# Padding 32 bytes shorter and a stated place for the first weight sums, in a transformer layer on one core

## The chip, the cores and the metric

The kernel runs on one core of one Trainium2 chip. The metric is the device time of one execution in microseconds (us); lower is better. The engines are named PE (matrix products; PEld is its loading of weights), DVE, ACT and POOL (elementwise work), and SP, which here only issues transfers.

## The reference

One decoder layer over 512 tokens of width 2048, all in float32:

```python
h = rmsnorm(x, norm_attn_g)
proj = h @ w_in                      # q, k, v of two attention groups
o_a = swa_attention(rmsnorm(q_a), rmsnorm(k_a), v_a, sinks, rel_bias)
o_b = stick_breaking_attention(q_b, k_b, v_b)
mix = concat(rmsnorm(o_a, swa_out_g), rmsnorm(o_b, sb_out_g))
x = x + mix @ w_out                  # 2048 x 2048
h = rmsnorm(x, norm_mlp_g)
u = h @ w_up                         # 2048 x 8192
x = x + square(relu(u)) @ w_down     # 8192 x 2048
```

## The kernel before

**Products.** Each float32 operand is split into two parts, hi (the value cast to float32r, on ACT, L91) and lo (the rest, a subtraction of two tiles on DVE, L92). A product is then three matmuls, hi by hi, hi by lo and lo by hi. A matmul has two operands in on-chip memory: 128 columns of weights, which PE loads first, and a moving operand of 256 or 512 columns.

**Stages.** Projection of k and v, then q, k and v of the two attention groups, with the attention itself worked in between; the output projection; the up projection (from 741 us); the down projection (from 1407 us). In all projections ahead of the up projection a matmul has 512 moving columns, and there are 2,496 of them (nine groups of 192, eight of 96).

**Up projection.** 32 column groups, each of 8 steps: steps 0 to 6 have 21 matmuls, step 7 has 24, 171 in all (L809 to L811), with 256 moving columns. Weights are `hi_u`, `lo_u`; the moving operand is `h2h`, `h2l`, one pair of tiles for each step. POOL sums columns of the raw weights `st_u` into `s_u` (L779), four instructions for two steps (fast matrix products need such sums). DVE makes `lo_u` from `st_u` and `s_u`, and does most of `u_finish` of the group before (L823 to L845), in program order. PE, DVE and POOL each run their instructions in the order written.

**Down projection.** 16 turns (`cj`), each of 7 products of 24 matmuls with 512 moving columns (L1053 to L1055), 2,688 in all. Weights are `ad`, the moving operand is `hi_d`, `lo_d`. POOL makes four sums of raw weights for a turn, T1 to T4, each in two halves (L931). Half of the tiles of `st_d`, and T1 of turn 0, are asked for in the last column group of the up projection:

```python
if k == 1:
    d_load(0, 0)
    d_act(0, ORDER[0])
elif k == 4:
    d_sum(0, "T1")
elif k == 6:
    d_split(0)
```

The other `ad` of turn 0 are issued on SP behind the stores of the group before (`ac<-ah`, `ac<-al`, L848), the second of which needs `al` (L845).

**Where tiles lie.** On-chip memory is a stack from the left (pools `const`, `wst`, `whl`, `sm`, `big`, later `aba`, `rwa`, `ew`) and one from the right (`once` to `wk` in attention, `h2_0` to `h2_5`, `sp`, later `rwb`, `t3`, `abb`). Small tiles of the pool `const` come first on the left, and tiles that nothing uses (`pad_left`, `pad_small`, `pad_right`) set where the large ones begin. In the built program before, the large tiles on the left begin 32 bytes past a multiple of 512 in each partition (the first of `wst` at 3104), those on the right at a multiple of 512. So:

- projections ahead of the up projection: both operands on the left, both 32 past;
- up projection: weights on the left (32 past); `h2` of steps 0 to 5 on the right (0), of steps 6 and 7 on the left (32 past);
- down projection: moving operand on the left (32 past); `ad` of the first product of each turn on the left (32 past, pool `aba`), of the other six on the right (0, pool `abb`);
- `mp_k` (L338, L339): weights `bo` in `const`, 32 past, and moving operands on the right (0).

Slices of these operands begin at multiples of 512 bytes in their tiles.

Of the kernel before, what the change touches and what calls it, by code (L numbers as in the profile page):

```python
# [12 lines left out]
F32 = mybir.dt.float32  # L13
# [7 lines left out]
P = 128  # L21
# [37 lines left out]
def hymba_layer(ctx: ExitStack, tc: tile.TileContext, x, norm_attn_g, w_in, q_norm_g, k_norm_g,  # L59
                sinks, rel_bias, swa_out_g, sb_out_g, w_out, norm_mlp_g, w_up, w_down, sel, eye, out):  # L60
    nc = tc.nc
    x, out = x[0], out[0]
# [4 lines left out]
    const = ctx.enter_context(tc.tile_pool(name="const", bufs=1))  # L67
# [293 lines left out]
        return o  # L361

    oscr = dram.tile([2 * 8, P, T], F32, name="oscr")
    const.tile([P, 32], F32, name="pad_left")
    sm.tile([P, 32], F32, tag="pad", bufs=1, name="pad_small")
    S = [once.tile([P, T], F32, name=f"S{b}") for b in range(2)]

# [389 lines left out]


    wu = w_up.rearrange("(k p) c -> p k c", p=P)
    raws, sums, parts_u = {}, {}, {}  # L760

    def u_load(i):
        if i < G * KP // 2:
# [5 lines left out]
    def u_sums(i):  # L769
        if i < G * KP // 2:  # L770
            w = raws[i]
            s_ = sp.tile([P, 2, 4, P], F32, tag="s", name=f"s_u{i}")
            if i % (KP // 2) == PLAIN // 2:
                w, s_ = w[:, 0:1], s_[:, 0:1]
            for o, a, b, op in ((s_[:, :, 0], w[:, :, 0], w[:, :, 2], ALU.add),
                                (s_[:, :, 2], w[:, :, 1], w[:, :, 0], ALU.subtract),
                                (s_[:, :, 1], s_[:, :, 0], w[:, :, 1], ALU.subtract),
                                (s_[:, :, 3], w[:, :, 3], s_[:, :, 1], ALU.subtract)):
                nc.gpsimd.tensor_tensor(out=o, in0=a, in1=b, op=op)  # L779
            sums[i] = s_  # L780

    def u_split(i):
# [68 lines left out]
    def u_step(i, ps, finishing):  # L851
        if i % 2 == 0:
            u_load(i // 2 + 4)
            u_sums(i // 2 + 2)
        u_split(i + 2)
        u_products(i, ps)
        if finishing is not None:
            next(finishing, None)

    def u_begin(c2):  # L860
        if c2 == 3:
            for i in range(4):
                u_load(i)
            u_sums(0)
            u_split(0)
            u_sums(1)
# [12 lines left out]
    def u_banks(g):  # L879
        pool, tag = ((pa, "pa"), (pp, "pp"))[g % 2]  # L880
        return [pool.tile([P, 512], F32, tag=tag, name=f"ps_u{g}{m}") for m in range(4)]
# [26 lines left out]
    def d_load(cj, r):  # L908
        if cj < 2 * NC:
            c, j = divmod(cj, 2)  # L910
            for h in range(2):
                pool = rwa if (4 * cj + 2 * r + h) % 6 < 2 else rwb
                st = pool.tile([P, 2, 1024], F32, tag="rw", name=f"st_d{cj}{r}{h}")
                nc.sync.dma_start(out=st, in_=wd[1 - r, :, 4 * c + 2 * h:4 * c + 2 * h + 2,
                                                 j * 1024:(j + 1) * 1024])
                for n in range(2):
                    raw[cj, f"B{r + 1}{n + 1}", h] = st[:, :, n * 512:(n + 1) * 512]

    def d_act(c, i):
        if c < NC:  # L920
            a = (aba if i == ORDER[0] else abb).tile([P, 2, 4, HP], F32R, tag="a", name=f"ad{c}{i}")
            nc.sync.dma_start(out=a.bitcast(F32), in_=ac[c][i])
            act[c, i] = a

    def d_sum(cj, name):
        if cj < 2 * NC:
            a, b = {"T1": ("B12", "B11"), "T2": ("B22", "T1"), "T3": ("B22", "B12"), "T4": ("B21", "T2")}[name]
            for h in range(2):
                pool, tag = (t3, "t3") if name == "T3" else (wst, "st")
                o = pool.tile([P, 2, 512], F32, tag=tag, name=f"{name}_{cj}{h}")  # L930
                nc.gpsimd.tensor_tensor(out=o, in0=raw[cj, a, h], in1=raw[cj, b, h], op=ALU.subtract)  # L931
                raw[cj, name, h] = o

    def d_split(q):
        if q < 14 * NC:
            cj, s = divmod(q, 7)
            for h in range(2):
                hi = whl.tile([P, 2, 512], F32R, tag="hi", name=f"hi_d{q}{h}")
                lo = whl.tile([P, 2, 512], F32R, tag="lo", name=f"lo_d{q}{h}")
                split(raw[cj, D_PRODUCTS[s][2], h], hi, lo)  # L940
                parts_d[q, h] = hi, lo
# [51 lines left out]
    for g in range(1, G):  # L993
        finishing = u_finish(g - 1, ps, ew)
        ps = u_banks(g)
        for k in range(KP):
            if g == G - 1:
                if k == 1:
                    d_load(0, 0)
                    d_act(0, ORDER[0])  # L1000
                elif k == 4:
                    d_sum(0, "T1")
                elif k == 6:
                    d_split(0)
            u_step(g * KP + k, ps, finishing)
# [6 lines left out]
    for cj in range(2 * NC):  # L1012
# [7 lines left out]
        for s, (name, ai, _, b, more) in enumerate(D_PRODUCTS):  # L1020
# [22 lines left out]
            a = act[c, ai]  # L1043

            at_end = q == 14 * NC - 1
            for h, tt in sorted(((h, tt) for h in range(2) for tt in range(2)), key=lambda x: x[::-1] if at_end else x):
                bh, bl = parts_d[q, h]
                ts = slice(tt * P, (tt + 1) * P)
                o = banks[b][tt]
# [39 lines left out]
```

## Time and profile before

| | |
|---|---|
| median of 3 runs | 2043.79 us (2041.43 to 2044.12) |
| the profiled execution | 2043.11 us, of which the span from first to last instruction is 2041.0 us |
| busy in the span | PE 2004.0, DVE 1626.8, POOL 1020.3, ACT 1014.5 us |
| mean granted PE clock | 0.996 |

The times are the kernel's whole device time; 2.1 us of the profiled one lie outside the span. Busy time of PE overlaps from one matmul to the next, so that a PE that is always busy can still run its matmuls at a slower or faster pitch (time from one start to the next).

### The profile page before, as it was taken

How to read it: one execution, taken by the hardware profiler on the slowest of the kernel's cores; microseconds unless marked ns; L12 is line 12 of the kernel's file. 1: busy time of each engine (PE TensorE's matmuls, PEld its weight loads, DVE VectorE, ACT ScalarE, POOL GpSimd, SP SyncE). 2: the span in 40 equal slices, each digit the busy share in tenths (PEclk: the TensorE clock that was granted, in tenths of full speed). 3: DMA queues.
4: the chain of work that ended last, by engine and by line, in shares of the span. 5: the costliest groups of instructions: out<-in, count | busy, mean ns of one | idle time of the engine just before them, and what ended most of it. 6: DMA issues, size and time to landing. Idle time of an engine off the chain costs nothing. (4 is left out here: it accounts for less than half of the span.)

```text
span 2041.0 us, 31132 instructions
## 1 busy us (share of the span) xinstructions
PE 2004.0 (98%) x11748; PEld 1725.3 (85%) x11748; DVE 1626.8 (80%) x2034; ACT 1014.5 (50%) x1676; POOL 1020.3 (50%) x904
## 2 busy tenths in 40 slices
PE   8999999999999999999999999998999999999998
PEld 7887787778677889999999999997788888888887
DVE  4378646665775578999999999998989999999987
ACT  6267534544553565555555555554543333333343
POOL 0014332222320127777777777775756556655654
PEclk9999999999999999999999999999999999999999
DMA  6742332223345555665656565656756557456351
GB/s 220 123 129 85 100 93 81 73 92 111 107 134 186 168 166 182 203 203 183 203 182 205 182 205 182 206 182 264 273 223 227 177 216 267 155 226 258 145 186 62
DMA packets 213914, 350.30 MB, mean 172 GB/s; under 512 B 9779, under 2 KB 154372, under 8 KB 206596
## 3 DMA queue, kind: packets, MB, share of 16 engines
q1 hardware_dynamic: 211216, 345.02, 49.8%
q10 hardware_dynamic: 2548, 3.30, 1.3%
q8 instruction: 92, 1.51, 0.3%
q14 instruction: 58, 0.48, 0.1%
HBM read 270.16 MB, written 78.12 MB: 171 GB/s over the span
## 5 line engine op out<-in xcount | busy, mean ns | idle before, releaser
L811 PE MATMUL ps_u<-h2h,lo_u 128*128 128x256 f32 x1824 | 515.9, 283 | 6.3 <-DVE lo_u L92 6.3
L810 PE MATMUL ps_u<-h2l,hi_u 128*128 128x256 f32 x1824 | 514.7, 282 | 2.4 <-DVE h2l L92 2.4
L809 PE MATMUL ps_u<-h2h,hi_u 128*128 128x256 f32 x1824 | 514.8, 282 | 0.1
L1053 PE MATMUL ps_d<-hi_d,ad 128*128 128x512 f32 x896 | 353.4, 394 | 3.4 <-ACT U L969 1.6
L1054 PE MATMUL ps_d<-lo_d,ad 128*128 128x512 f32 x896 | 353.4, 394 | 1.2 <-DVE lo_d L92 1.2
L1055 PE MATMUL ps_d<-hi_d,ad 128*128 128x512 f32 x896 | 353.2, 394 | 0.0
L811 PEld LDWEIGHTS ps_u<-h2h,lo_u 128*128 128x128 f32 x1824 | 346.7, 190 | 7.5 <-DVE lo_u L92 6.7
L810 PEld LDWEIGHTS ps_u<-h2l,hi_u 128*128 128x128 f32 x1824 | 346.6, 190 | 2.9 <-DVE h2l L92 2.8
L809 PEld LDWEIGHTS ps_u<-h2h,hi_u 128*128 128x128 f32 x1824 | 346.6, 190 | 0.3 <-ACT h2h L91 0.3
L779 POOL TENSOR_TENSOR s_u<-st_u 128x256 f32<-128x256 f32 (+1 forms) x256 | 200.1, 801 | 252.3 <-DVE lo_u L92 181.2
L92 DVE TENSOR_TENSOR lo_d<-T,hi_d 128x1024 fp32r<-128x1024 f32 x128 | 241.4, 1899 | 38.1 <-ACT hi_d L91 37.4
L931 POOL TENSOR_TENSOR T<-st_d,T 128x1024 f32<-128x1024 f32 x64 | 169.1, 2645 | 201.0 <-DVE lo_d L92 198.5
L91 ACT CAST hi_d<-T 128x1024 fp32r<-128x1024 f32 x128 | 134.4, 1051 | 203.0 <-PE ps_d L1055 177.6
L92 DVE TENSOR_TENSOR lo_u<-st_u,hi_u 128x384 fp32r<-128x384 f32 (+1 forms) x256 | 218.2, 853 | 4.4 <-ACT hi_u L91 4.3
L1053 PEld LDWEIGHTS ps_d<-hi_d,ad 128*128 128x128 f32 x896 | 167.9, 187 | 44.6 <-ACT U L969 2.1
L92 DVE TENSOR_TENSOR lo_d<-st_d,hi_d 128x1024 fp32r<-128x1024 f32 x96 | 193.5, 2028 | 13.7 <-ACT hi_d L91 13.2
L1054 PEld LDWEIGHTS ps_d<-lo_d,ad 128*128 128x128 f32 x896 | 168.0, 188 | 42.0 <-DVE lo_d L92 2.0
L1055 PEld LDWEIGHTS ps_d<-hi_d,ad 128*128 128x128 f32 x896 | 168.0, 187 | 40.1
L92 DVE TENSOR_TENSOR lo_u<-s_u,hi_u 128x512 fp32r<-128x512 f32 x224 | 178.1, 795 | 1.0 <-ACT hi_u L91 1.0
L91 ACT CAST hi_u<-s_u 128x512 fp32r<-128x512 f32 x224 | 138.5, 618 | 78.7 <-POOL s_u L779 78.6
L91 ACT CAST hi_d<-st_d 128x1024 fp32r<-128x1024 f32 x96 | 100.6, 1050 | 152.2 <-PE ps_d L1055 140.6
L779 POOL TENSOR_TENSOR s_u<-st_u,s_u 128x256 f32<-128x256 f32 (+1 forms) x128 | 167.8, 1311 | 10.0
(223 smaller groups left out, 3825.7 us busy)
## 6 DMA issues: line engine op xcount, KB each, us to landing
st_u<-in_w_up SPq DMA_DIRECT2D x128, 512.0 KB, 4.5
st_d<-in_w_down SPq DMA_DIRECT2D x64, 1024.0 KB, 8.3
ad<-ac SPq DMA_DIRECT2D x56, 1024.0 KB, 5.1
ac<-ah SPq DMA_DIRECT2D x32, 896.0 KB, 6.3
ac<-al SPq DMA_DIRECT2D x32, 896.0 KB, 6.6
st_qk<-in_w_in SPq DMA_DIRECT2D x64, 256.0 KB, 3.0
st_o<-in_w_out SPq DMA_DIRECT2D x32, 512.0 KB, 4.5
st_qa<-in_w_in SPq DMA_DIRECT2D x16, 512.0 KB, 4.1
```

Source lines behind the costliest of these rows:

```text
L91: nc.scalar.copy(out=hi, in_=st)
L92: nc.vector.tensor_tensor(out=lo, in0=st, in1=hi.bitcast(F32), op=ALU.subtract)
L779: nc.gpsimd.tensor_tensor(out=o, in0=a, in1=b, op=op)
L809: nc.tensor.matmul(o, wh[:, a], hh[:, b], start=first, stop=False, skip_group_check=True)
L810: nc.tensor.matmul(o, wh[:, a], hl[:, b], start=False, stop=False, skip_group_check=True)
L811: nc.tensor.matmul(o, wl[:, a], hh[:, b], start=False, stop=(k == KP - 1), skip_group_check=True)
L931: nc.gpsimd.tensor_tensor(out=o, in0=raw[cj, a, h], in1=raw[cj, b, h], op=ALU.subtract)
L1053: nc.tensor.matmul(o, al, bh[:, kk], start=first, stop=False, skip_group_check=True)
L1054: nc.tensor.matmul(o, al, bl[:, kk], start=False, stop=False, skip_group_check=True)
L1055: nc.tensor.matmul(o, ar, bh[:, kk], start=False, stop=end, skip_group_check=True)
```

## The change

```diff
-    const.tile([P, 32], F32, name="pad_left")
+    const.tile([P, 24], F32, name="pad_left")
...
-    raws, sums, parts_u = {}, {}, {}
+    raws, sums, parts_u, last_sum = {}, {}, {}, [None]
...
-                nc.gpsimd.tensor_tensor(out=o, in0=a, in1=b, op=op)
+                last_sum[0] = nc.gpsimd.tensor_tensor(out=o, in0=a, in1=b, op=op)
...
                 elif k == 4:
-                    d_sum(0, "T1")
+                    with tc.issue_after(last_sum[0].ins):
+                        d_sum(0, "T1")
```

The pad has 24 words in place of 32. Every tile of the left stack behind it lies 32 bytes lower: the first of `wst` at 3072, and all large tiles, left and right, begin at multiples of 512. `bo` lies ahead of the pad and stays. The number of instructions of each engine stays the same.

The second part moves two instructions on POOL. Below is POOL's order in the last column group; `s_u126` and `s_u127` are the sums for steps 4 and 5, and 6 and 7, of that group; T1_00 and T1_01 are the halves of T1 of turn 0.

```order
-L931 TENSOR_TENSOR T1_00_15576<-st_d000_15477 128x1024
 L779 TENSOR_TENSOR s_u126_15440<-st_u126_15303 128x2x128 x2
 L779 TENSOR_TENSOR s_u126_15440<-s_u126_15440,st_u126_15303 128x2x128
 L779 TENSOR_TENSOR s_u126_15440<-st_u126_15303,s_u126_15440 128x2x128
-L931 TENSOR_TENSOR T1_01_15578<-st_d001_15479 128x1024
 L779 TENSOR_TENSOR s_u127_15511<-st_u127_15369 128x128 x2
 L779 TENSOR_TENSOR s_u127_15511<-s_u127_15511,st_u127_15369 128x128
 L779 TENSOR_TENSOR s_u127_15511<-st_u127_15369,s_u127_15511 128x128
+L931 TENSOR_TENSOR T1_00_15576<-st_d000_15477 128x1024
+L931 TENSOR_TENSOR T1_01_15578<-st_d001_15479 128x1024
 L931 TENSOR_TENSOR T3_00_15731<-st_d010_15713,st_d000_15477 128x1024
 L931 TENSOR_TENSOR T2_00_15820<-st_d010_15713,T1_00_15576 128x1024
```

The two halves of T1 stood ahead of the sums of steps 4 and 5 and ahead of those of step 6; now both stand behind them, and T3 and T2 follow directly.

ACT keeps its order; two of its casts for the second product of the down projection get one more wait:

```order
 L91 CAST hi_d00_15639<-st_d000_15477 128x1024 [waits PE_49]
 L91 CAST hi_d01_15643<-st_d001_15479 128x1024 [waits PE_49]
-L91 CAST hi_d10_15735<-T1_00_15576 128x1024 [waits PE_49,Activation_49]
-L91 CAST hi_d11_15739<-T1_01_15578 128x1024 [waits DVE_49,PE_49]
+L91 CAST hi_d10_15735<-T1_00_15576 128x1024 [waits PE_49,Activation_49,Pool_49]
+L91 CAST hi_d11_15739<-T1_01_15578 128x1024 [waits DVE_49,PE_49,Pool_49]
 L822 COPY p1_31_15769<-ps_u310_15436 128x256 [waits PE_49]
 L91 CAST hi_d20_15824<-T3_00_15731 128x1024 [waits DVE_49,PE_49,Pool_49]
```

`hi_d10` and `hi_d11` now wait for POOL by name. On PE, DVE, ACT and SP each instruction stands where it stood.

## Rows read from the trace of the kernel before

**Rows 1.** Windows of 100 us: busy us and instructions (x) of each engine, granted PE clock.

```profile
core 0: us, PE busy (x) PEld busy (x) DVE busy (x) ACT busy (x) POOL busy (x), PEclk, DMA share, GB/s
...
800.00:900.00 100.00, 100.00 (x845) 100.00 (x844) 90.46 (x123) 58.09 (x95) 74.58 (x79) 1.00 0.64 208
...
1200.00:1300.00 100.00, 100.00 (x838) 99.59 (x837) 90.45 (x123) 56.23 (x94) 74.17 (x77) 1.00 0.59 191
...
1700.00:1800.00 100.00, 100.00 (x431) 80.61 (x430) 93.64 (x77) 37.84 (x36) 55.89 (x20) 1.00 0.62 230
```

**Rows 2.** Timeline of PE, down projection: start, length; 24 matmuls from row to row.

```profile
1605.31 0.39 PE L1053 MATMUL ps_d<-hi_d,ad 128*128 128x512 f32 x1
...
1610.76 0.39 PE L1053 MATMUL ps_d<-hi_d,ad 128*128 128x512 f32 x1
...
1616.36 0.39 PE L1053 MATMUL ps_d<-hi_d,ad 128*128 128x512 f32 x1
```

**Rows 3.** Timeline of PE, up projection, column group 10: firsts of steps 0, 6, 7, next.

```profile
948.95 0.28 PE L809 MATMUL ps_u<-h2h,hi_u 128*128 128x256 f32 x1
...
963.86 0.28 PE L809 MATMUL ps_u<-h2h,hi_u 128*128 128x256 f32 x1
...
966.37 0.28 PE L809 MATMUL ps_u<-h2h,hi_u 128*128 128x256 f32 x1
...
969.25 0.28 PE L809 MATMUL ps_u<-h2h,hi_u 128*128 128x256 f32 x1
```

**Rows 4.** Timeline of PE: first of the four matmuls of mp_k, and the next after them.

```profile
71.25 0.40 PE L338 MATMUL mp_k<-sh_k,bo 128*128 128x512 f32 x1
...
72.19 0.39 PE L116 MATMUL ps_qa<-hT,hi_qa 128*128 128x512 f32 x1
```

**Rows 5.** Timeline of PE, q and k projection; 28 matmuls from the first to the second.

```profile
470.62 0.39 PE L117 MATMUL ps_qk<-hT,hi_qk 128*128 128x512 f32 x1
...
476.97 0.39 PE L118 MATMUL ps_qk<-hT,lo_qk 128*128 128x512 f32 x1
```

**Rows 6.** Timeline of PE where the projections meet; in brackets idle time and its releaser.

```profile
1376.73 0.28 PE L809 MATMUL ps_u<-h2h,hi_u 128*128 128x256 f32 x1
...
1388.10 0.38 PE L811 MATMUL ps_u<-h2h,lo_u 128*128 128x256 f32 x1 [0.89 <-DVE lo_u L92]
...
1392.94 0.28 PE L809 MATMUL ps_u<-h2h,hi_u 128*128 128x256 f32 x1
...
1398.73 0.58 PE L811 MATMUL ps_u<-h2h,lo_u 128*128 128x256 f32 x1 [5.40 <-DVE lo_u L92]
...
1404.64 0.28 PE L811 MATMUL ps_u<-h2h,lo_u 128*128 128x256 f32 x1
...
1406.55 0.40 PE L1053 MATMUL ps_d<-hi_d,ad 128*128 128x512 f32 x1
...
1413.58 0.47 PE L1053 MATMUL ps_d<-hi_d,ad 128*128 128x512 f32 x1 [1.41 <-DMA ad<-ac]
```

**Rows 7.** Timeline of POOL, same place: the two halves of T3.

```profile
1390.44 2.86 POOL L931 TENSOR_TENSOR T<-st_d,st_d 128x1024 f32<-128x1024 f32 x1
...
1395.75 2.52 POOL L931 TENSOR_TENSOR T<-st_d,st_d 128x1024 f32<-128x1024 f32 x1
```

**Rows 8.** Timeline of DVE, same place: three of its subtractions.

```profile
1377.49 0.55 DVE L92 TENSOR_TENSOR lo_u<-st_u,hi_u 128x384 fp32r<-128x384 f32 x1
...
1395.99 2.69 DVE L92 TENSOR_TENSOR lo_u<-st_u,hi_u 128x384 fp32r<-128x384 f32 x1
...
1401.87 3.22 DVE L845 TENSOR_TENSOR al<-a,ah 128x1792 fp32r<-128x1792 f32 x1 [1.20 <-ACT ah L843]
```

**Rows 9.** Timeline of SP, same place: DMA issues.

```profile
1384.41 0.89 SPq L914 DMA_DIRECT2D st_d<-in_w_down  x2
...
1405.58 4.26 SPq L922 DMA_DIRECT2D ad<-ac  x6
```

**Rows 10.** Waits over the whole span: us in total, times, longest us.

```profile
ACT hi_d L91 <- PE ps_d L1055: 318.2, 189, 1.8
```

## The prediction

> **What bounds the kernel.** I read the windows of 100 us first. In the up projection (800 to 1300 us) and in the down projection (1700 to 1800 us) PE is busy 100.00 of 100.00 us at a granted clock of 1.00, DVE 90 and 94 us, POOL 74 and 56 us [rows 1]. So time can change there only if PE's matmuls get another pitch, or if a helper falls behind. The number of matmuls in 100 us does change: 845 from 800 us on, 838 from 1200 us on, which says that something other than PE's own pitch counts by then.
>
> So I read the pitch itself from PE's timeline, and set it beside where the two operands lie. In the down projection the first product of a turn, both operands 32 bytes past a multiple of 512, takes 5.45 us for 24 matmuls, 227 ns each; the next, moving operand 32 past and weights at 0, takes 5.60 us, 233.3 ns [rows 2]. `mp_k` is the other way round, weights 32 past and moving operand at 0: 0.94 us for four, about 234 ns [rows 4]. The q and k projection, both 32 past, takes 6.35 us for 28, 227 ns [rows 5]. In the up projection, with 256 columns, steps 0 to 5 (weights 32 past, moving operand at 0) take 14.91 us for 126 matmuls, 118.3 ns; steps 6 and 7, both 32 past, take 2.51 us for 21 and 2.88 us for 24, 120 ns [rows 3].
>
> One reading fits all four: what counts is whether weights and moving operand lie equally far past a multiple of 512. With 512 columns equal is 6.3 ns faster than unequal, whichever of the two is off; with 256 columns equal is 1.7 ns slower. No row has both at 0 in a full-size matmul of this kind, which is the gap in the evidence. And every unequal pair here is also a pair of one tile on the left and one on the right of the memory, so the sides could be the cause instead of the offset.
>
> **Down projection.** After the change all these operands are at multiples of 512, so equal. Six of seven products in each of 16 turns go from 5.60 to 5.45 us: 96 x 0.15 = 14.4 us. Can the helpers follow? DVE is busy 94% of a turn, which would be 96% of a shorter one; but ACT waits 318 us for PE to give back `hi_d` buffers [rows 10], so the helpers run ahead and PE holds them back. I take it that they follow. In the first turn PE waits for transfers, and in the last two for the last additions; there (18 of the 96 products, 2.7 us) I count half. Term: -13.1 us, bounds -14.4 and 0 (the sides, not the offset).
>
> **Up projection.** Steps 0 to 5 go from 118.3 to 120 ns. A group then takes 171 x 0.120 = 20.52 us in place of 20.30 [rows 3]; for 31 groups that is +6.8 us. But 838 matmuls in the window from 1200 us on are a pitch of about 119.6 ns (two of the 838 lie across its edges), or 20.45 us for a group: there PE no longer sets the pace, the chain through POOL and DVE does [rows 1]. PE at 20.30 us has eaten 0.15 us of the chain's lead in each group, and once the lead is gone, for some 10 groups, it waits those 0.15 us. These 1.5 us are not paid twice. Term: +5.2 us, bounds 0 and +6.8. With PE at 20.52 us the chain keeps its lead, 0.15 us in each of some 20 groups at the least: 3 to 5 us in the last group. That matters next.
>
> **Where the projections meet.** From the start of the last group at 1376.73 us to the second product of the down projection at 1413.58 us, 36.85 us go by [rows 6]. Undisturbed it would be 20.52 + 5.45 = 25.97 us, so 10.9 us are lost: 0.89 and 5.40 us of waiting for `lo_u`; 2.7 us in 27 matmuls after the longer wait, which take 219 ns each, from 1398.73 to 1404.64 us; and 1.41 us of waiting for `ad`, with the small remainder in between.
>
> The cause of the long wait is on POOL and DVE. A T sum takes some 2.5 us, and a DVE subtraction that meets one takes as long: a `lo_u` of 0.55 us took 2.69 us beside T3 [rows 7, 8]. PE went on when that `lo_u` ended, at 1398.68 us, 0.4 us after the second half of T3.
>
> The moved halves of T1 stop delaying the sums of steps 4 to 6. But they then stand in one row with T3 and T2: five sums of some 2.5 us from about 1385.5 us on (where the sums of step 6 end if they are not delayed, by the group before), which end at about 1398 us, where T3 ends now. In that row DVE gets through about one subtraction for each sum, and it has five to make: `lo_u` of step 5 twice, two of `u_finish`, `lo_u` of step 6. So the move alone gives nothing that I can price: 0, bounds -2 and +2 (a subtraction more or less in the row). The wait for T1 that two casts of ACT get costs nothing: T1 ends at about 1390 us, and the casts feed PE's second product, at 1413.58 us. If it were late, `p1`, the next casts and that product would be queued behind it.
>
> The lead is worth more. PE starts the last group about 5 us later, POOL and DVE do not, so T1 runs while PE is in steps 1 to 3. T3 needs the second half of `st_d`, which SP asks for at 1384.41 us, when PE leaves step 2, 7.6 us into the group; it had landed by 1390.44 us, when T3 began [rows 7, 9]. Between the end of T1 and that landing DVE is free to finish `lo_u` of step 6, and perhaps of step 7. I count through both ends. With a lead of 3 us step 6 is in time, `lo_u` of step 7 meets T2 and T3 and is 3 us late, and `ad`, which SP issues from 1405.58 us on, behind the store of `al` that ends at 1405.09 us [rows 8, 9], lands as before: the second product starts at 1413. With a lead of 5 us there is no stall in the up projection, `al` ends some 6 us earlier, and under 1 us is spent waiting for `lo_d`: it starts at 1408 to 1409. I take 1410.5. Counted from the later start of the last group, 8.2 of the 10.9 us are given back. Term: -8.2 us, bounds -10.4 and -5.1.
>
> **Sum.** 2043.1 (the profiled execution: span 2041.0 and 2.1 outside) - 13.1 + 5.2 - 8.2 = 2027.0 us. The median of the runs shown is 0.7 us above the profiled one: 2027.7, say 2027.5 us. These runs lie within 0.13%; about 0.2%, 4 us, can be told from no change.
>
> **Rival: the offset is nothing to PE.** The sides of the memory, or something else that goes with them, set the pitch. Then the 14.4 us stay where they are, the up projection keeps its pace, and only the moved T1 is left: 2041 to 2046 us. For it: sides and offsets go together in every row. Against it: across the sides 512 columns are slower and 256 columns faster, which the sides alone don't explain. Chance 0.13. The trace shows 5.45 beside 5.60 us for the same work [rows 2]. The Trainium skill (SBUF — State Buffer, "Who interferes with whom") speaks for this rival: by it PE has two read ports, one for the moving operand and one for loading weights, independent of each other, and PE never waits on anyone; the sum would be the 2043 us of before. The trace does not agree as far as the pair's place changes the pitch.
>
> **Rival on the other side: equal at 0 is not like equal at 32.** If two streams from multiples of 512 meet as badly as unequal ones do, 233.3 ns become the pitch of every matmul with 512 columns. The 2,496 of the projections ahead and the 384 of the first products get 6.3 ns each, +18 us, and the down projection wins nothing; with +5.2 and -8.2, or with neither, that is 2058 to 2061 us. It decides from a pitch of about 230.5 ns on, where 2,880 matmuls lose what 2,304 and the other two terms win. Against it: no row shows that the common offset matters. Chance 0.08.
>
> **Rival: the pitch falls, but little comes of it.** The last group stalls as before (-5.1 in place of -8.2), and DVE at 96% is late in the down projection and takes back half of 13.1: 2036.7 us, 2033 to 2040. Against it: the 318 us that ACT waits for PE. Chance 0.16.
>
> **Rival: equal at 0 is better still**, 220 ns or less: 5,184 matmuls x 7 ns are 36 us more, of which the helpers let some through: 2000 to 2018 us. Chance 0.05.
>
> **Numbers.** The forecast has 0.58: 2027.5 us, by itself 2020 to 2033. The range reaches to the third rival and most of the first: 2018 to 2044 us. Faster by over 0.2% are the forecast, the last two rivals and a small part of the first (a gain by the move alone): 0.81. Within 0.2% is the rest of the first: 0.11. Slower is the second: 0.08.
>
> **What would show it.** In the timeline of PE: every product of a steady turn at 5.45 us, a turn at 38.1 in place of 39.0 us; a group of the up projection at 20.5 us, and about 835 matmuls in each of its windows from first to last; the q and k projection still at 227 ns. In the last group no wait of 5 us for `lo_u`, and the second product of the down projection at about 1410 us. The prediction is wrong if products two to seven stay at 5.60 us, if the q and k projection slows down, or if DVE shows up as PE's releaser in the middle of the down projection.

## The result and the profile after

The changed kernel takes 2031.94 us (median of 4 runs, 2028.76 to 2032.30), the kernel before on the same chip 2043.39 us (4 runs, 2041.43 to 2044.12). The ratio is 0.9942, 95% interval 0.9925 to 0.9959: faster by 0.6%, 4.4 us more than the 2027.5 us forecast, inside the range. The profiled execution took 2031.77 us, with a span of 2029.7 us.

First the windows of the changed kernel: three of 100 us that answer to [rows 1], and three stages (up projection to the start of its last group; from there to the second product of the down projection; turns 1 to 13). The columns are those of [rows 1].

```profile
800.00:900.00 100.00, 100.00 (x836) 100.00 (x835) 87.68 (x123) 57.50 (x94) 75.12 (x79) 1.00 0.64 208
1200.00:1300.00 100.00, 100.00 (x835) 100.00 (x835) 87.69 (x123) 56.92 (x92) 74.09 (x79) 1.00 0.59 188
1700.00:1800.00 100.00, 100.00 (x442) 82.80 (x442) 97.07 (x80) 38.70 (x37) 57.52 (x21) 1.00 0.65 247
...
741.54:1382.47 640.93, 638.60 (x5319) 638.00 (x5317) 560.45 (x780) 366.71 (x604) 468.85 (x494) 1.00 0.60 193
1382.47:1416.38 33.91, 29.11 (x197) 27.00 (x196) 32.70 (x29) 13.84 (x19) 27.95 (x15) 0.90 0.61 228
...
1450.93:1945.97 495.04, 495.04 (x2185) 410.05 (x2184) 473.18 (x370) 200.39 (x197) 302.90 (x105) 1.00 0.58 217
```

The up projection runs at one pace from its second group to the last but one (836 and 835 matmuls in 100 us, 845 and 838 before), slower than before at its start. The down projection gets 442 matmuls into 100 us in place of 431, and DVE follows at 97%.

Then PE's timeline of the changed kernel, the places of [rows 5], [rows 3], [rows 6] and [rows 2] in order of time.

```profile
470.56 0.39 PE L117 MATMUL ps_qk<-hT,hi_qk 128*128 128x512 f32 x1
...
476.91 0.39 PE L118 MATMUL ps_qk<-hT,lo_qk 128*128 128x512 f32 x1
...
951.55 0.28 PE L809 MATMUL ps_u<-h2h,hi_u 128*128 128x256 f32 x1
...
966.67 0.28 PE L809 MATMUL ps_u<-h2h,hi_u 128*128 128x256 f32 x1
...
972.07 0.28 PE L809 MATMUL ps_u<-h2h,hi_u 128*128 128x256 f32 x1
...
1401.00 0.39 PE L811 MATMUL ps_u<-h2h,lo_u 128*128 128x256 f32 x1 [0.49 <-DVE lo_u L92]
...
1403.73 0.39 PE L1054 MATMUL ps_d<-hi_d,ad 128*128 128x512 f32 x1
1408.43 0.80 PE L1055 MATMUL ps_d<-lo_d,ad 128*128 128x512 f32 x1 [4.31 <-DVE lo_d L92]
...
1413.72 0.51 PE L1055 MATMUL ps_d<-lo_d,ad 128*128 128x512 f32 x1
...
1416.38 0.39 PE L1054 MATMUL ps_d<-hi_d,ad 128*128 128x512 f32 x1
...
1603.25 0.39 PE L1054 MATMUL ps_d<-hi_d,ad 128*128 128x512 f32 x1
...
1608.69 0.39 PE L1054 MATMUL ps_d<-hi_d,ad 128*128 128x512 f32 x1
...
1614.13 0.39 PE L1054 MATMUL ps_d<-hi_d,ad 128*128 128x512 f32 x1
```

Read from the bottom: first and second product of a turn now take the same 5.44 us, 226.7 ns a matmul (5.45 and 5.60 before). In column group 10 the 126 matmuls of steps 0 to 5 take 15.12 us, 120.0 ns each (14.91 us before). The q and k projection stays at 6.35 us for 28. In the last group the wait of 5.40 us for `lo_u` is down to 0.49 us, but a wait of 4.31 us for `lo_d` stands behind the first matmul of the down projection. After it the granted clock is 0.50 for some 5 us (1.2 GHz), and matmuls of 512 columns follow each other by 427 ns; twelve of them take 5.29 us, 2.6 us more than at 227 ns. The kernel before lost 2.7 us in the same way after its wait of 5.40 us, at a granted clock of 0.50 too.

A ledger of both profiled executions, in us, by the starts of first matmuls, shows where 11.3 us went (the times of the first row differ by more between two executions of the changed kernel, 741.54 and 739.93 us):

| stretch | before | after | difference |
|---|---|---|---|
| up to the up projection | 740.86 | 741.54 | +0.7 |
| up projection to the start of its last group | 635.87 | 640.93 | +5.1 |
| meeting place: from there to the second product | 36.85 | 33.91 | -2.9 |
| rest of turn 0 | 35.57 | 34.55 | -1.0 |
| turns 1 to 13 | 507.52 | 495.04 | -12.5 |
| turns 14 and 15, end | 84.33 | 83.73 | -0.6 |

The meeting place on the helpers, answers to [rows 7], [rows 8] and [rows 9]: timeline of POOL, of DVE and of SP in the changed kernel.

```profile
1395.26 2.58 POOL L931 TENSOR_TENSOR T<-st_d,st_d 128x1024 f32<-128x1024 f32 x1 [2.30 <-DVE lo_u L92]
1397.81 2.58 POOL L931 TENSOR_TENSOR T<-st_d,T 128x1024 f32<-128x1024 f32 x1
1400.35 2.87 POOL L931 TENSOR_TENSOR T<-st_d,st_d 128x1024 f32<-128x1024 f32 x1
1403.16 4.14 POOL L931 TENSOR_TENSOR T<-st_d,T 128x1024 f32<-128x1024 f32 x1
```

```profile
1395.17 0.41 DVE L837 TENSOR_TENSOR a<-a 128x256 f32<-128x256 f32 x1
1395.62 2.51 DVE L840 TENSOR_TENSOR a<-a 128x256 f32<-128x256 f32 x1
1398.05 2.89 DVE L92 TENSOR_TENSOR lo_u<-st_u,hi_u 128x512 fp32r<-128x512 f32 x1
1400.86 4.23 DVE L845 TENSOR_TENSOR al<-a,ah 128x1792 fp32r<-128x1792 f32 x1
1405.02 4.49 DVE L92 TENSOR_TENSOR lo_d<-st_d,hi_d 128x1024 fp32r<-128x1024 f32 x2
```

```profile
1390.10 0.89 SPq L914 DMA_DIRECT2D st_d<-in_w_down  x2
...
1405.12 0.37 SPq L848 DMA_DIRECT2D ac<-al  x1
1405.59 3.82 SPq L922 DMA_DIRECT2D ad<-ac  x6
```

SP asks for the second half of `st_d` when PE leaves step 2. PE is 5.7 us later there than before, and so is the request: 1390.10 in place of 1384.41 us. So T3 starts at 1395.26 in place of 1390.44 us. (Its row names DVE as the releaser, the row of a second execution below names PE. What sets the time is the transfer: three executions below (padding alone, the changed kernel again, T3 held), with the request at 1388.39, 1388.47 and 1389.27 us, begin the first sum that reads it 5.2, 5.1 and 5.0 us later. Here it is 5.2, and the row of the last of the three names the transfer.) From there four sums (T3 and T2, two halves each) stand in a row until 1407.3 us. Beside them L840 takes 2.51 us, the last `lo_u` 2.89, `al` 4.23 and the two halves of `lo_d` together 4.49; L837, a subtraction of the same size as L840 that started 0.09 us before T3, took 0.41. `al` ends at 1405.09 us, as before to the hundredth by the clock of the execution, 0.7 us earlier if one counts from the start of the up projection, and SP issues `ad` when it did before, at 1405.59 us. The wait went from `lo_u` to `lo_d`, and little of the time came back. The Trainium skill (SBUF — State Buffer, "Who interferes with whom") says that a DVE instruction with two inputs in SBUF contends with a GpSimd instruction that reads SBUF; this trace agrees: 0.41 us where the subtraction started ahead of the sum, 2.51 us beside it.

### The profile page after: what moved, and what is told of

The parts are those of the page before. It is cut to its first block, busy times and chain, and to the rows that moved or that the text cites. A ratio compares the mean times of both kernels' runs of the same rounds, so it can differ in the third digit from the quotient of the medians.

```text
span 2029.7 us, 31133 instructions
## 1 busy us (share of the span) xinstructions
PE 1995.5 (98%) x11748; PEld 1731.1 (85%) x11748; DVE 1612.1 (79%) x2034; ACT 1017.8 (50%) x1676; POOL 1024.0 (50%) x904
## 5 line engine op out<-in xcount | busy, mean ns | idle before, releaser
L1054 PE MATMUL ps_d<-hi_d,ad 128*128 128x512 f32 x896 | 349.8, 390 | 2.8 <-ACT U L969 1.6
L1056 PE MATMUL ps_d<-hi_d,ad 128*128 128x512 f32 x896 | 349.6, 390 | 0.0
L91 ACT CAST hi_u<-st_u 128x384 fp32r<-128x384 f32 (+1 forms) x256 | 134.0, 524 | 221.3 <-PE ps_u L810 131.1
L92 DVE TENSOR_TENSOR lo_u<-st_u,hi_u 128x384 fp32r<-128x384 f32 (+1 forms) x256 | 200.6, 784 | 19.8 <-ACT hi_u L91 19.8
```

The source lines that it names most:

```text
L91: nc.scalar.copy(out=hi, in_=st)
L92: nc.vector.tensor_tensor(out=lo, in0=st, in1=hi.bitcast(F32), op=ALU.subtract)
L1054: nc.tensor.matmul(o, al, bh[:, kk], start=first, stop=False, skip_group_check=True)
L1056: nc.tensor.matmul(o, ar, bh[:, kk], start=False, stop=end, skip_group_check=True)
```

## The experiments

All of them change the kernel at the places shown; no run leaves out a part of the computation. "Before" is the kernel before on the same chip in the same session. The stretches of the ledger, for the runs that a text below speaks of (up: the up projection to its last group; meeting; their sum; turns 1 to 13):

| run | up | meeting | sum | turns 1 to 13 |
|---|---|---|---|---|
| before | 635.87 | 36.85 | 672.72 | 507.52 |
| after | 640.93 | 33.91 | 674.84 | 495.04 |
| changed kernel again | 640.90 | 31.77 | 672.67 | 495.66 |
| padding alone | 640.94 | 33.63 | 674.57 | 495.99 |
| both sides 32 past | 640.92 | 32.91 | 673.83 | 495.04 |
| left side 64 past | 637.80 | 37.53 | 675.33 | 499.62 |
| left side 256 past | 640.98 | 31.33 | 672.31 | 495.66 |
| move alone | 635.99 | 36.87 | 672.86 | 507.55 |
| up projection unequal | 635.96 | 36.22 | 672.18 | 495.89 |
| T3 held | 640.94 | 28.57 | 669.51 | 497.27 |
| T3 held by half | 640.93 | 27.97 | 668.90 | 495.15 |
| T3 held, up projection unequal | 635.81 | 31.99 | 667.80 | 497.15 |

Each row is one execution. Five of them have equal operands everywhere and no sum held off; their meeting places take 31.33 to 33.91 us, which is how far executions of much the same kernel differ there.

**The padding alone.**

```diff
-                    with tc.issue_after(last_sum[0].ins):
-                        d_sum(0, "T1")
+                    d_sum(0, "T1")
```

> Only the padding is shortened (all operands at multiples of 512); the halves of T1 stay where they were on POOL, among the sums of the last group of the up projection. Theory (the relative place of the two operands sets PE's pitch, the moved T1 is worth nothing): pitches as in the changed kernel, 227 ns in every product of the down projection and 120.0 ns in every step of the up projection; time 2030 to 2034 us beside 2031.9 of the changed kernel. Rival (the stated order is worth something of its own now that PE comes later to the last group): 2036 to 2042 us, with a wait of 3 us or more for lo_u in the last group.

2032.36 us (2030.88 to 2034.43), ratio to before 0.9951 (0.9938 to 0.9963): the whole change within what can be told. The rival's sign was there all the same, in PE's timeline:

```profile
1402.23 0.58 PE L811 MATMUL ps_u<-h2h,lo_u 128*128 128x256 f32 x1 [3.44 <-DVE lo_u L92]
...
1414.38 0.47 PE L1053 MATMUL ps_d<-hi_d,ad 128*128 128x512 f32 x1 [0.80 <-DMA ad<-ac]
```

Without the move PE waits 3.44 us for `lo_u`, with it 4.31 us for `lo_d`; the meeting place takes 33.63 and 33.91 us (31.77 in a second execution with the move). The move shifts the wait, and what it pays, if anything, is within what executions differ by.

**The move alone.**

```diff
-    const.tile([P, 24], F32, name="pad_left")
+    const.tile([P, 32], F32, name="pad_left")
```

> Only T1 is moved behind the last weight sums of the up projection; the padding is as before (left side 32 bytes past a multiple of 512, right side at 0). Theory: pitches as before, 233.3 ns in products two to seven and 118.3 ns in steps 0 to 5; the long wait for lo_u stays in some form, time 2041 to 2046 us. Rival (the move brings the gain): 2031 to 2036 us.

2042.38 us, ratio 1.0000 (0.9991 to 1.0009). The pitches are those of before (5.60 us, 118.3 ns), and the last group still has a wait of 5.93 us for `lo_u`. The theory holds; the gain is the padding's.

**Both sides 32 bytes past; and the two sides swapped.** The first kernel has both edits, so that both sides lie 32 bytes past a multiple of 512; the swapped one has only the first edit, on the right.

```diff
-    edge.tile([P, 120], F32, name="pad_right")
+    edge.tile([P, 112], F32, name="pad_right")
-    const.tile([P, 24], F32, name="pad_left")
+    const.tile([P, 32], F32, name="pad_left")
```

> The changed kernel with both sides 32 bytes past a multiple of 512 in place of both at 0. Theory (equal is what counts, the common offset nothing): 227 ns in all products, 120.0 ns in all steps, 2030 to 2034 us. Rival (the sides of the memory set the pitch and the change gained by reaching 0): 233.3 and 118.3 ns, 2041 to 2046 us. Second rival (one of the operands has to lie at a multiple of 512): every pitch unequal to 227, over 2041 us.

> The changed kernel with the left side at multiples of 512 and the right side 32 bytes past: the two offsets are swapped against the kernel before. Theory: unequal again, 233.3 ns in products two to seven, 118.3 ns in steps 0 to 5, 227 ns in the projections ahead whose two operands lie on one side; 2040 to 2046 us. Rival (the left side's place alone counts, weights and moving tile of the changed kernel win because the left side is at 0): 227 and 120.0 ns, 2030 to 2034 us.

Both sides 32 past: 2032.43 us, ratio 0.9948 (0.9936 to 0.9961). Swapped: 2043.69 us, 1.0007 (0.9999 to 1.0016). The windows of 1200 and 1700 us, first of the kernel with both 32 past, then of the swapped one:

```profile
1200.00:1300.00 100.00, 100.00 (x836) 100.00 (x835) 87.15 (x122) 57.17 (x93) 75.83 (x80) 1.00 0.59 188
1700.00:1800.00 100.00, 100.00 (x443) 82.81 (x442) 97.13 (x82) 39.06 (x37) 57.53 (x21) 1.00 0.65 247
```

```profile
1200.00:1300.00 100.00, 99.62 (x838) 98.60 (x837) 90.46 (x122) 56.02 (x93) 74.02 (x78) 1.00 0.59 191
1700.00:1800.00 100.00, 100.00 (x432) 80.74 (x431) 93.36 (x79) 37.41 (x37) 55.16 (x21) 1.00 0.62 233
```

With no operand at a multiple of 512 but both equally far past, the down projection has its 443 matmuls; with one at 0 and one at 32, whichever, 432. `mp_k`, whose weights lie on the left and whose moving operand lies on the right in every kernel, says the same: its four matmuls take 0.91 us with both 32 past, 0.94 us before [rows 4]. It is the relative place, not the sides and not the multiple.

**How far apart.** The left side is moved to 64, 128 or 256 bytes past a multiple of 512, the right stays at 0 (`pad_left` of 40, 56 and 88 words); one run of each.

> The changed kernel with the left side 64 bytes past a multiple of 512, the right side at 0. Theory: if the pair must agree modulo 64, pitches as changed (227 and 120.0 ns) and about 2032 us; if it must agree modulo more than 64, 233.3 and 118.3 ns and about 2043 us. No preference ahead of the run.

> The changed kernel with the left side 128 bytes past a multiple of 512, the right side at 0. Both 32 and 64 bytes apart changed the pitches (118.3 and 233.3 ns; 113 and 229 ns), 256 did not. If agreement modulo 128 is what counts: 120 and 227 ns, 2030 to 2034 us. If only modulo 256 is: another pair of pitches, up to 2043 us.

> The changed kernel with the left side 256 bytes past a multiple of 512, the right side at 0. If the pair must agree modulo 512, 233.3 and 118.3 ns and about 2043 us; if agreement modulo 256 or less is enough, 227 and 120.0 ns and about 2032 us. Read with the run at 64 bytes.

They took 2038.60, 2039.85 and 2030.47 us. Pitches in undisturbed stretches (a step of the up projection, a product of the down projection over its 24):

| weights and moving operand apart | 256 columns | 512 columns | kernels |
|---|---|---|---|
| 0 | 120.0 ns | 226.7 ns | after, both 32 past |
| 256 bytes | 120.0 ns | 226.7 ns | left 256 |
| 32 bytes | 118.3 ns | 233.3 ns | before, move alone |
| 32 bytes, the other operand further | 117.8 ns | 233.3 ns | swapped |
| 64 bytes | 113.3 ns | 228.9 ns | left 64 |
| 128 bytes | 118.7 ns | 232.4 ns | left 128 |

So equality modulo 256 is enough. At 64 bytes neither of the two cases that were expected came: both pitches are new. In all rows but the swapped one it is the weights that lie further in the up projection, and the moving operand in the down projection; the other way round was run at 32 bytes only. The 113.3 ns at 64 bytes is the best pitch for the up projection, and brings little there: from the second group on its groups take 19.68 us, but about 20.53 us from the seventh on. Groups of PE's instructions by line in the up projection of that kernel (800 to 1300 us; busy, mean ns, idle time before them) show what holds them:

```profile
L811 PE MATMUL ps_u<-h2h,lo_u 128*128 128x256 f32 x1392 | 390.1, 280 | 12.0 <-DVE lo_u L92 11.9
```

The 12.0 us are some 0.55 us in nearly each of the groups of that window. By the starts, the first matmul that needs `lo_u` comes 0.84 us after the one ahead of it in place of 0.11, and the next one 0.22 us later: together almost all of the 0.85 us by which these groups are longer.

**The up projection unequal, the down projection equal.**

```diff
-            hi = whl.tile([P, 7, P], F32R, tag="hi", name=f"hi_u{i}")
-            lo = whl.tile([P, 7, P], F32R, tag="lo", name=f"lo_u{i}")
+            hi = whl.tile([P, 7 * P + 8], F32R, tag="hi", name=f"hi_u{i}")
+            lo = whl.tile([P, 7 * P + 8], F32R, tag="lo", name=f"lo_u{i}")
+            hi, lo = [t[:, 8:].rearrange("p (a c) -> p a c", a=7) for t in (hi, lo)]
```

> The changed kernel with hi_u and lo_u shifted 32 bytes within their buffers: the weights of the up projection lie 32 bytes past a multiple of 512, its moving operand at 0, so its pitch is the unequal one (118.3 ns in all steps), the down projection stays equal (227 ns). Theory (at 118.3 ns the chain through POOL and DVE bounds the up projection at about 20.45 us a group, and the lead of lo_u is used up): a group takes 20.24 us at first and about 20.45 later, the last group starts some 5 us earlier than in the changed kernel, a wait of 3 us or more for lo_u is back in it, and the time is 2028 to 2033 us. Rival (the dearer pitch of the up projection is a plain loss of 1.7 ns a matmul): 2024 to 2027 us.

2030.44 us (2028.31 to 2032.31), ratio 0.9936 (0.9923 to 0.9950): no different from the changed kernel. Groups take 20.24 us from the second to the fourteenth and 20.46 us from the sixteenth on; the lead of `lo_u` at the start of a group falls to 0.1 us by then. The last group starts 5 us sooner than in the changed kernel, and PE's timeline has the long wait back:

```profile
1398.38 0.58 PE L812 MATMUL ps_u<-h2h,lo_u 128*128 128x256 f32 x1 [5.93 <-DVE lo_u L92]
...
1412.49 0.47 PE L1055 MATMUL ps_d<-hi_d,ad 128*128 128x512 f32 x1 [1.04 <-DMA ad<-ac]
```

From the start of the up projection to the second product it takes 672.18 us, the kernel before 672.72, the changed one 674.84 and 672.67. What PE wins in the up projection it waits for at the meeting place, and the other way round.

**T3 held off.** If the sums of POOL beside `al` and `lo_d` are what costs, holding T3 of the first turn until `lo_d` is done must bring the second product forward. A small extra addition on POOL that reads `lo_d` does that:

```diff
-    const.tile([P, 24], F32, name="pad_left")
+    pad_left = const.tile([P, 24], F32, name="pad_left")
...
-                d_sum(cj, "T3")
+                if cj == 0:
+                    low = parts_d[0, 1][1].bitcast(F32)[:, 0, 0:16]
+                    held = nc.gpsimd.tensor_tensor(out=pad_left[:, 0:16], in0=low, in1=low, op=ALU.add)
+                    with tc.issue_after(held.ins):
+                        d_sum(cj, "T3")
+                else:
+                    d_sum(cj, "T3")
```

> The changed kernel with T3 and T2 of the first turn held off on POOL: a small extra addition (16 columns) that reads lo_d of the first product's second half stands ahead of T3, so that DVE meets no sum of POOL while it does the last lo_u, al and lo_d. Theory (after the change the stall at the meeting place sits in al and lo_d, which DVE does beside T3 and T2): al ends at about 1400 us in place of 1405, the 4.3 us wait for lo_d goes, the first product takes near 6 us in place of 12.65, the second starts at 1406 to 1410 us, and the time is 2023 to 2027 us. Rival (the second product waits for a transfer or for T3 and T2 themselves, now later): 2030 to 2036 us, with the wait moved to product two or three.

2029.30 us (2026.27 to 2032.47), ratio 0.9929 (0.9916 to 0.9941). The edit holds T3 only, not T2 as the text above has it: the halves of T2 now run ahead of the extra addition. Timeline of POOL (the halves of T2, then the extra addition and T3), of DVE and of PE in this kernel, and the window of its meeting place with the columns of [rows 1]:

```profile
1394.27 2.42 POOL L931 TENSOR_TENSOR T<-st_d,T 128x1024 f32<-128x1024 f32 x1 [2.13 <-DMA st_d<-in_w_down]
1398.16 2.40 POOL L931 TENSOR_TENSOR T<-st_d,T 128x1024 f32<-128x1024 f32 x1 [1.48 <-DVE lo_u L92]
1404.80 1.13 POOL L1027 TENSOR_TENSOR pad_left<-lo_d 128x16 f32<-128x16 f32 x1 [4.23 <-DVE lo_d L92]
1405.89 5.71 POOL L931 TENSOR_TENSOR T<-st_d,st_d 128x1024 f32<-128x1024 f32 x2
```

```profile
1397.00 0.42 DVE L840 TENSOR_TENSOR a<-a 128x256 f32<-128x256 f32 x1
1397.34 0.69 DVE L92 TENSOR_TENSOR lo_u<-st_u,hi_u 128x512 fp32r<-128x512 f32 x1
1399.23 3.22 DVE L845 TENSOR_TENSOR al<-a,ah 128x1792 fp32r<-128x1792 f32 x1 [1.20 <-ACT ah L843]
1402.37 2.35 DVE L92 TENSOR_TENSOR lo_d<-st_d,hi_d 128x1024 fp32r<-128x1024 f32 x2
```

```profile
1403.63 0.50 PE L1061 MATMUL ps_d<-lo_d,ad 128*128 128x512 f32 x1 [1.08 <-DVE lo_d L92]
...
1410.20 0.47 PE L1060 MATMUL ps_d<-hi_d,ad 128*128 128x512 f32 x1 [1.06 <-DMA ad<-ac]
```

```profile
1381.63:1410.20 28.57, 26.43 (x197) 24.87 (x196) 25.83 (x28) 13.71 (x19) 20.57 (x14) 1.00 0.61 217
```

With two sums in the row in place of four, L840 and `lo_u`, beside which POOL does nothing, take 0.42 and 0.69 us, `al`, beside one sum, 3.22, and the halves of `lo_d` 1.2 us each. The meeting place takes 28.57 us, 5.3 less than in the first execution of the changed kernel and less than in any of the five that hold nothing off: the mechanism is shown. About half of the 5.3 us is shorter waiting. The other half is the clock: the window's granted clock is 1.00 here and 0.90 in the changed kernel, which had twelve matmuls at half clock behind its long wait, 2.6 us.

The expectation asked for more. The wait for `lo_d` fell to 1.08 us and did not go, the first product takes 8.0 us and not 6, and `al` ends at 1402.45 us and not at 1400: one sum still lies on it, which makes it 3.22 us long, where it takes 2.03 us in the hold by half below, with no sum beside it. The time is not what was expected either (2023 to 2027 us), and its spread overlaps that of the changed kernel. Some 2 us are given back: in turn 1 PE waits three times 0.3 us for `lo_d`, and two products take 6.37 and 6.68 us in place of 5.44. The granted clock is 1.00 there; that it fell, as the second expectation below says, is not so. That the late `lo_d` of turn 1 comes from the later T3 is likely, but was not tested by itself.

**Three more on one chip:** the changed kernel again; T3 held until the first half of `lo_d` is done (`parts_d[0, 0]` in place of `parts_d[0, 1]`); T3 held as above together with the shifted `hi_u` and `lo_u`.

> The changed kernel once more, on the same chip as the two that hold T3 off, so that they can be compared directly: 2030 to 2033 us by every theory. In its profile the second product starts 31 to 34 us after the last group of the up projection, depending on which instruction of DVE meets which sum of POOL.

> As the run that holds T3 off until lo_d of the first product is done, but the extra addition reads the first half of lo_d, so T3 comes about 1 us earlier. Theory (the hold gained 5 us at the meeting place and gave 2 us back in the second turn, where lo_d came a third of a us late three times and the granted clock fell): the give-back shrinks a little, 2026 to 2030 us. Rival (T3 now meets the second half of lo_d, which then takes 2.4 us in place of 1.2): 2029 to 2032 us.

> T3 of the first turn held off as in the run before, and hi_u and lo_u shifted by 32 bytes as well, so that the up projection has the unequal pitch. Theory (the chain through POOL and DVE paces the up projection at 20.45 us a group from the middle on, and ends the last group's sums about 2 us earlier than where PE takes 20.52): the last group starts some 5 us earlier, PE waits 3 to 5 us in it for lo_u, the second product starts 2 us earlier than with the hold alone, 2025 to 2029 us. Rival (a late chain also delays T1 and al by as much): no gain over the hold alone, 2028 to 2031 us.

They took 2030.12 us (2028.27 to 2031.42; ratio 0.9933, 0.9921 to 0.9946), 2029.05 us (0.9933, 0.9920 to 0.9947) and 2026.96 us (2026.07 to 2029.13; 0.9920, 0.9907 to 0.9934). Against this execution of the changed kernel the hold by half shortens the meeting place by 3.8 us and gives 1.6 us back in turn 0; the first hold, which ran on another chip, shortens it by 3.2 us and gives 1.6 us back in turn 1. So the give-back moved and did not shrink, and the second half of `lo_d` took 1.2 us, not the 2.4 of the rival; the time of 2029.05 us decides for neither. In the last kernel the second product comes 1.7 us sooner after the start of the up projection than with the first hold and 1.1 us sooner than with the hold by half (2 us were expected), and PE waits 0.4 and 1.6 us for `lo_u` in the last group, less than the 3 to 5 us expected. It has the lowest median of all, 3.2 us below the changed kernel on the same chip; the intervals of the two ratios overlap, so that it beats the kernel before is measured, and that it beats the changed one is not.

The changed kernel again differs from the first profile at the meeting place, 31.77 in place of 33.91 us. POOL, DVE and PE there (timeline of this second execution):

```profile
1393.60 2.40 POOL L931 TENSOR_TENSOR T<-st_d,st_d 128x1024 f32<-128x1024 f32 x1 [2.17 <-PE ps_u L811]
```

```profile
1393.64 2.63 DVE L837 TENSOR_TENSOR a<-a 128x256 f32<-128x256 f32 x1
1396.31 2.50 DVE L840 TENSOR_TENSOR a<-a 128x256 f32<-128x256 f32 x1
```

```profile
1401.63 0.58 PE L811 MATMUL ps_u<-h2h,lo_u 128*128 128x256 f32 x1 [2.75 <-DVE lo_u L92]
```

In the first profile L837 started 0.09 us before T3 and took 0.41 us; here it started 0.04 us after T3 and took 2.63. The whole row of DVE stands one place later against the sums, PE waits 2.75 us for `lo_u` in step 7 (third view) and not at all for `lo_d`. Two more profiles fall the same way: with both sides 32 past L837 started 0.10 us before T3, took 0.42 us, and the meeting place took 32.91 us; with the left side 256 past it started after T3, took 2.62 us, and the meeting place took 31.33. Which of the two starts first goes with 1 to 2.6 us there, in these four executions.

## Why the prediction was right, and where it was off

**Direction and mechanism: right.** What counts is whether weights and moving operand lie equally far past a multiple of 512 (256 is enough, as the runs show). The gap named in the evidence, both at 0, is closed by the changed kernel (226.7 and 120.0 ns), and the sides are excluded by the two kernels with the right side at 32. So the first rival falls: the pair's relative place moved the pitch of 512 columns from 226.7 to 233.3 ns at the same granted clock of 1.00. The Trainium skill (SBUF — State Buffer, "Who interferes with whom"), weighed there, says that PE's two read ports are independent and that PE never waits on anyone; the runs do not bear out what the rival drew from it, that the place of the two operands is nothing to PE. Whether the ports or something else in the memory cause it, no run shows. The rival on the other side and "better still" fall with the same 226.7 ns.

**Down projection, -13.1: right, slightly small.** The last three rows of the first ledger sum to -14.1 us, near the bound of -14.4; DVE at 97% did follow. Every product of turns 1 to 13 takes 5.44 us, and PE waits for `lo_d` nowhere in them (in the second execution once, 0.3 us, in turn 1). So of the third rival only the first half came true, the stall in the last group.

**Up projection, +5.2: right as a stage (+5.1), but not a cost by itself.** The groups from the second to the last but one take 20.52 us, as forecast, and `lo_u` comes 3.2 to 3.5 us ahead of the matmul that needs it at the start of each group from the third to the last; in the kernel before this lead fell from 2.95 us in the third group to 0.06 in the twenty-third, as the working had it. The unequal variant gives the 5 us back to PE, and the second product comes no sooner than in the second execution of the changed kernel (672.18 and 672.67 us). Up projection and meeting place are two parts of one stretch that POOL, DVE and the transfers pace: in every run without a hold that the table shows it takes 672 to 675 us, whatever the pitch. The working saw the tie, but priced its second part by a lead of 3 to 5 us.

**Meeting place, -8.2: the step that failed; it measured -2.9 us.** The second product was to start at 1410.5 us and started at 1416.38. That figure was the middle of two ends, a lead of 3 us (1413 us, -5.1) and one of 5 us (1408 to 1409 us). The lead was 3.2 to 3.5 us, near the lower end, and the second execution came out as that end has it: step 7 waits 2.75 us for `lo_u`, and the meeting place gains 5.1 us. In the first execution even that was not reached. Of the upper end, where "there is no stall in the up projection, `al` ends some 6 us earlier, and under 1 us is spent waiting for `lo_d`", it had the first clause (0.49 us) and not the others: `al` ended at 1405.09 us, 0.7 us earlier at most, and the wait for `lo_d` was 4.31 us, with matmuls at half clock after it.

The working had seen that SP's request for `st_d` hangs on PE leaving step 2, and used it only for the free time ahead of T3. It did not carry the delay on: T3 and T2, whose data is asked for 5.7 us later, then lie on `al` and `lo_d`. Holding T3 off gave -8.3 us against before (28.57 us): about the size that was forecast, by an edit that the forecast did not have, so that the likeness of the two numbers is luck. It shows that the sums beside `al` and `lo_d` were most of what was missing. The sum of both terms was to be -3.0 us; it was +2.1 in one execution and 0.0 in the other. With the +0.7 us ahead of the up projection, less than two executions of the changed kernel differ by there (1.6 us), the ledger adds up: -14.1 + 5.1 - 2.9 + 0.7 = -11.2, to rounding the 11.3 us of the spans, where the terms had -16.1.

**Moved T1, 0: right,** by both kernels with one part alone (padding alone 2032.36 us beside 2031.94; move alone at ratio 1.0000).

## What to carry to other kernels

Look up where the two operands of a matmul lie in a partition, and compare them with each other; in this kernel a few bytes of padding among small tiles were worth 3% of the matmul pitch, with another sign for 256 than for 512 columns. A faster pitch pays only where PE is the last to be ready: in the stage that a chain of helpers paces, 113 ns and 120 ns brought the second product of the down projection at about the same time (675.3 and 672.7 to 674.8 us from the start of the up projection). When a stage begins later, ask for every transfer whose request hangs on it where its followers will then lie, and what they will meet.

## What was not expected of the hardware

The pitch is no simple function of the distance: for 256 columns 120.0, 118.3, 113.3, 118.7 and 120.0 ns at 0, 32, 64, 128 and 256 bytes, for 512 columns 226.7, 233.3, 228.9, 232.4 and 226.7 ns. Of the distances run, equal operands are the best case of 512 columns and the worst of 256.
